# One encoder layer in split fp32: the order of the first down product, the place of X loads, and the step of a norm

## Chip, core and metric

The kernel runs on one core of a Trainium2 chip, as one launch. The metric is device time in microseconds: the median of the runs of one kernel. A profile of one execution lies beside it.

## The reference, cut to what matters

One layer is computed for 1024 prompt frames and 32 sample frames together (T = 1056 rows of width 1024): normalisation and projections, windowed attention and a gated recurrence, a mix, and then the part that this change touches:

```
[a | u] = RMSNorm(x) @ W_up            # 1024 -> 2 x 2816
a = causal depthwise conv3(a)
x = x + RMSNorm((gelu(a) * u) @ W_down)    # 2816 -> 1024, the "down product"
x = x + (p @ W_ple) * sigmoid(x @ W_ple_gate)
```

All of it is fp32. The kernel multiplies each pair of fp32 operands as a rounded high part and the rest: three matmuls (high by high, high by low, low by high) add up in one PSUM accumulator.

## The kernel before

The down product is worked out by Strassen's scheme: seven products (`i` = 0 to 6) of half-size blocks instead of eight. The operand of the product `i` that holds activations is called X(i); its sums were written to DRAM tiles `td` by the up stage. X(i) has three chunks (`KC`: 4, 4 and 3 blocks of 128 rows, index `j`), each in two halves `p` of 264 columns. A chunk's half is loaded by `x_in(i, q)` (q = 2j + p, one DMA on SyncE's queue, L1846) into a page of SBUF and then split by `x_parts`: ScalarE rounds it to the high part (L1835), VectorE subtracts (L1836). The pages of X(i) were those of X(i-2), so a load must wait until TensorE is done with these.

A product has four column blocks `c` of the output. A *step* is one (c, j): for both halves, 3 matmuls for each of the 4 or 3 blocks, so 24 or 18 matmuls (L2058 to L2060). Twelve steps make a product, 84 the whole stage (`QS`, counted as q). The results of a column block add up in one tile `st` of two PSUM banks, of which there are three; two more banks (`tr_bank`) serve transposes and small sums. In products 1 to 6 the steps go by c, and by j within c. In product 0 they go (0,0) (0,1) (1,0) (1,1) (2,0) (2,1), then the third chunk of blocks 0, 1 and 2, then the three steps of block 3: three `st` tiles allow three blocks to wait at a time. The third chunk of X(0) holds one k block that only the last up unit produces. It doesn't go through DRAM: VectorE computes it (L1696), and two DMAs on SyncE's queue copy it into place (L1698).

Each step needs weights. `w_in_(q)` loads one or two blocks of W_down (L1870; two in products 1 to 5), `w_parts(q)` adds the two on VectorE (L1877) and splits them as above into `wd`. In the program the load stands six steps ahead of its use and the split three. Raw weights of even q have two buffers (`wr`); those of odd q share eight (`wb`) with the split weights.

After block c, `d_out` adds or copies the result into the accumulators `acc` (ScalarE L1910, L1911, L1914; VectorE L1907). In product 4 `square` squares the finished blocks and adds them up on VectorE (`sqd`, L1937). Then `x2_first(t)`, t counted from product 5's step 0, does the norm of the first half of the columns: `x2_norm` (t = 3) sums the squares over partitions by twelve matmuls of one column (L1948) and takes the reciprocal root in a chain of small VectorE operations (L1949, L213 to L219); `x2_rows` (t = 7) turns the root into rows by six transposes (L303). Loads, sums and splits of the next stage's operand follow for t = 7 to 20.

The order is made by a planner: each instruction has the priority of its place in the program, and an instruction whose operands and buffers are free in the plan may be issued ahead of earlier ones that are not. On the chip each engine's queue, SyncE's for the DMAs included, then goes strictly in the planned order. `behind(e)` holds what is traced inside it behind the last instruction of engine e traced before; the call under it adds this tie only to instructions of that same engine:

```
ins = next(i for i in reversed(nc.cur_bb.bb.instructions) if i.engine == e.engine)
st.enter_context(tc.issue_after(ins))
```

After the seven products comes the gate stage (L2168 on), in which `y_start` loads a block of the per-layer input, `pl` (L2086).

Of the kernel before, what the change touches and what calls it, by code (L numbers as in the profile page):

```python
# [10 lines left out]
F32 = mybir.dt.float32  # L11
# [6 lines left out]
P = 128  # L18
# [12 lines left out]
H = 264  # L31
# [28 lines left out]
def layer_kernel(  # L60
# [17 lines left out]
    def nm(s):  # L78
        n_names[0] += 1
        return f"{s}_{n_names[0]}"  # L80
# [4 lines left out]
    dma, gdma = nc.sync.dma_start, nc.gpsimd.dma_start  # L85
    V, S, G, E = nc.vector, nc.scalar, nc.gpsimd, nc.tensor

    def behind(*engines):

        st = ExitStack()  # L90
        for e in engines:
            ins = next(i for i in reversed(nc.cur_bb.bb.instructions) if i.engine == e.engine)
            st.enter_context(tc.issue_after(ins))
        return st
# [29 lines left out]
    ple_d = dp.tile([P, 8, T], F32, name="ple_d")  # L124
# [115 lines left out]
    def tr_bank():  # L240
        return bank(pp, "tr", 2)
# [1436 lines left out]
    def down_parts(f, a, ab, out):  # L1678

        k, o4 = f // 2, halves(out)  # L1680
        neg = a[:, 0:T].rearrange("p (b a c) -> p b a c", b=2, a=2)[:, 0]
        b1, b2 = o4[:, :, 0, :], o4[:, :, 1, :]
        if f % 2 == 0:
            to_td(0, k, b1)
            to_td(3, k, b1)
            if f < NF - 2:
                S.mul(neg, b1, -1.0)
                to_td(2, k, neg)
            to_td(5, k, b1)
            to_td(6, k, b2)  # L1690
            add_td(5, k, b2)
            return
        if f == NF - 1:
            e1 = halves(Up[0][:, 0, :].bitcast(F32))[:, :, 0, :]
            d = a[:, 0:T].rearrange("p (b a c) -> p b a c", b=2, a=2)[:, 1]
            V.tensor_tensor(d, b1, e1, op=ALU.subtract)  # L1696
            for p in range(2):
                dma(X[0, p, 2][:, 1, 2, :].bitcast(F32), d[:, p])  # L1698
        S.mul(neg, b2, -1.0)
        to_td(1, k, b2)  # L1700
        to_td(4, k, b2)
        if f < NF - 1:
            add_td(2, k, b1)
        add_td(3, k, b2)
        add_td(4, k, b1)
        add_td(6, k, neg)
# [131 lines left out]
    X = {}  # L1838

    def x_in(i, q):  # L1840
        j, p = divmod(q, 2)
        n = KC[j][1]
        t = X[i, p, j] = page_at(SETS[i % 2][q], [P, 2, 4, H], "X")
        if (i, j) == (0, 2):
            n -= 1
        dma(t[:, 1, 0:n, :].bitcast(F32), td[TDI[i]][j][:, p, 0:n, :])  # L1846

    def x_parts(i, q):
        j, p = divmod(q, 2)
        to_parts(X[i, p, j], KC[j][1])  # L1850
# [4 lines left out]
          (A12, A22, ALU.subtract), (A21, A11, ALU.subtract), (A11,))  # L1855
    NQ = 84
    W = {}
    first_q = [(c, j) for c in range(3) for j in range(2)] + [(c, 2) for c in range(3)] + [(3, j) for j in range(3)]
    QS = [(i, c, j) for i in range(7)
          for c, j in (first_q if i == 0 else [(c, j) for c in range(4) for j in range(3)])]  # L1860

# [10 lines left out]
    def w_parts(q):  # L1872
# [3 lines left out]
        if len(WS[i]) > 1:  # L1876
            V.tensor_tensor(src, src, raw[:, 1, 0:n, :], op=WS[i][2])  # L1877
        to_parts(t, n, src)

    AHEAD_IN, AHEAD_PARTS = 6, 3  # L1880
    DOWN_AT = {0: [lambda: x_in(0, 0), lambda: x_in(0, 1)],
               1: [lambda: w_in_(1), lambda: x_in(0, 2), lambda: x_in(0, 3)],
               2: [lambda: w_in_(3), lambda: x_in(0, 4), lambda: x_in(0, 5), lambda: w_parts(0)],
# [18 lines left out]
    def d_out(i, c, b):  # L1902

        to = {k: a[:, c] for k, a in acc.items()}

        def add(key, op):
            V.tensor_tensor(to[key], to[key], b, op=op)  # L1907

        if i == 0:
            S.copy(to[0, 1], b)  # L1910
            S.copy(to[0, 0], b)  # L1911
        elif i == 1:
            add((0, 1), ALU.add)
            S.mul(to[1, 1], b, -1.0)  # L1914
        elif i == 2:
            add((0, 0), ALU.subtract)
            S.copy(to[1, 0], b)
        elif i == 3:
            add((0, 0), ALU.add)
            add((1, 1), ALU.add)  # L1920
        elif i == 4:
            add((0, 0), ALU.add)
        else:
            if i == 6:
                add((1, 0), ALU.add)
            add((1, 1), ALU.add)
# [36 lines left out]
    def cols_of(t, k, h):  # L1963
        return halves(t[:, k, :])[:, :, h, :]
# [20 lines left out]

    def x2_first(t):

        if t == 3:
            x2_norm(0)
        if t == 7:  # L1990
            with behind(E):
                x2_rows(0)
        if 7 <= t < 15:
            x2_load(0, t - 7)
        if 9 <= t < 17:
            x2_sum(0, t - 9)
        if 13 <= t < 21:
            x2_split(0, t - 13)
# [24 lines left out]
    for i in range(7):  # L2023
        for s, key in ACC_AT.get(i, ()):
            acc[key] = acc_page(s, "acc")
        bs = {}
        for s in range(12):
            q = 12 * i + s
            c, j = QS[q][1:]
            n = KC[j][1]  # L2030
            if j == 0:
                bs[c] = pf.tile([P, 2, 512], F32, tag="st", name=nm("st"), bufs=3)
            b = bs[c]
            if q == 1:
                finish_up()
                fctx.close()
                foctx.close()
                ep = ctx.enter_context(right("ep"))
            a = 4 if i == 0 else 0
            if i < 6 and a <= s < a + 6:  # L2040
                x_in(i + 1, s - a)
            if q + AHEAD_PARTS < NQ:
                w_parts(q + AHEAD_PARTS)
            if q + AHEAD_IN < NQ:
                w_in_(q + AHEAD_IN)
            if i == 0 and s in (4, 5):
                x_parts(0, s)
            a = 6 if i == 0 else 5
            if i < 6 and a <= s < a + 6:
                with behind(V) if i == 0 else ExitStack(), behind(S) if i == 0 else ExitStack():  # L2050
                    x_parts(i + 1, s - a)
            w = W.pop(q)
            for p in range(2):
                x = X[i, p, j]
                for k in range(n):
                    o = b[:, p, 0:H]
                    first, last = j == 0 and k == 0, j == 2 and k == n - 1
                    E.matmul(o, w[:, 0, k, :], x[:, 0, k, :], start=first, stop=False)  # L2058
                    E.matmul(o, w[:, 0, k, :], x[:, 1, k, :], start=False, stop=False)  # L2059
                    E.matmul(o, w[:, 1, k, :], x[:, 0, k, :], start=False, stop=last)  # L2060
            if i == 6:
                last_product(s)
            if i > 4:
                x2_first(12 * (i - 5) + s)
            if j < 2:
                continue
            d_out(i, c, bs.pop(c)[:, :, 0:H])
            if i == 2:
                square(0, 4 + c)
            elif i == 4:  # L2070
                square(0, c)
            elif i == 6:
                square(1, c)
                square(1, 4 + c)
# [8 lines left out]
    def y_start(h, c):  # L2083
        y = ep.tile([P, 2, H], F32, tag="t", name=nm("y"), bufs=4)
        pl = ep.tile([P, 2, H], F32, tag="pl", name=nm("pl"), bufs=2)
        dma(pl[:], cols_of(ple_d, c, h))  # L2086
        return y, pl

    def y_out(h, c, b, y, pl, z):
# [155 lines left out]
```

## Time and profile before

| | us |
|---|---|
| runs | 1988.96, 1985.16, 1987.40 |
| median | 1987.4 |
| the profiled execution's own time | 1984.17 |
| its span, first to last instruction | 1982.4 |
| TensorE's matmuls busy | 1947.6 |
| weight loads of TensorE busy | 1925.4 |
| VectorE busy | 1469.6 |
| ScalarE busy | 973.5 |
| down products (matmuls of L2058 to L2060) | 1631.28 to 1871.4 |

The profile's times are those of one execution, which is 3.2 us below the median of the runs. The down products take up 240 us near the end, and the gate stage the last 111. Two of the views need a word. A row of the timeline gives the start, the duration, engine, line, operation, what is written and read, and the form; in brackets stands the idle time of the engine before it and what ended it. A row of the stretches gives the busy time of each engine with the count of its instructions, then the granted clock of TensorE as a share of 2.4 GHz, the busy share of the 16 DMA engines, and what they moved.

### The profile page before, as it was taken

Reading aid. Unit: us, or ns where it says so; the run is one execution under the profiler, and the core shown is the slowest. Engines: PE = TensorE matmul, PEld = TensorE weight load, DVE = VectorE, ACT = ScalarE, POOL = GpSimd, SP = SyncE. Lnnn points to the kernel's source line nnn. Section 1 sums busy time; section 2 is a strip of 40 time slices with the busy share of each in tenths; the row PEclk is TensorE's granted clock in tenths of the full one; section 3 lists DMA queues with packets and bytes.
Section 4 is the critical chain, followed back from the end, with each engine's and each line's share of the span. In section 5 each row is a group of like instructions: output and inputs, shape, how many; then the busy total and the mean of one; then the engine's idle time right before and its main releaser. Section 6 shows DMA issues by size and latency. Waiting matters only on the chain. (4 is left out here: it accounts for less than half of the span.)

```text
span 1982.4 us, 38678 instructions
## 1 busy us (share of the span) xinstructions
PE 1947.6 (98%) x14715; PEld 1925.4 (97%) x14715; DVE 1469.6 (74%) x3194; ACT 973.5 (49%) x2207; POOL 289.6 (15%) x442
## 2 busy tenths in 40 slices
PE   7999999999999999999999999999999999999998
PEld 6999999999999999999999999999999999999998
DVE  6888888688888888553455778877788786678752
ACT  6655556556666666542124754333333335444432
POOL 2010100000000000002100013444554420000000
PEclk9999999999999999999999999999999999999999
DMA  9322311411111111377656693656465579889443
GB/s 270 105 84 84 104 62 54 154 47 58 38 54 42 50 55 57 122 238 228 188 169 212 212 316 99 140 125 143 112 138 134 129 189 275 239 259 278 137 116 83
DMA packets 334767, 277.58 MB, mean 140 GB/s; under 512 B 15925, under 2 KB 318136, under 8 KB 333941
## 3 DMA queue, kind: packets, MB, share of 16 engines
q1 hardware_dynamic: 312655, 234.67, 39.5%
q0 software_dynamic: 21856, 40.38, 9.2%
q8 instruction: 115, 1.88, 0.4%
q14 instruction: 71, 0.58, 0.1%
q10 hardware_dynamic: 70, 0.06, 0.0%
HBM read 186.21 MB, written 88.57 MB: 139 GB/s over the span
## 5 line engine op out<-in xcount | busy, mean ns | idle before, releaser
L1751 PE MATMUL st<-op,wt 128*128 128x264 f32 x1232 | 350.2, 284 | 3.1 <-DVE nr L219 1.0
L1753 PE MATMUL st<-op,wt 128*128 128x264 f32 x1232 | 349.6, 284 | 0.0
L1752 PE MATMUL st<-op,wt 128*128 128x264 f32 x1232 | 347.9, 282 | 0.0
L1751 PEld LDWEIGHTS st<-op,wt 128*128 128x128 f32 x1232 | 231.2, 188 | 6.0 <-DVE Sp L1769 1.7
L1752 PEld LDWEIGHTS st<-op,wt 128*128 128x128 f32 x1232 | 231.4, 188 | 0.0
L1753 PEld LDWEIGHTS st<-op,wt 128*128 128x128 f32 x1232 | 230.9, 187 | 0.0
L2058 PE MATMUL st<-X,wd 128*128 128x264 f32 x616 | 176.7, 287 | 1.8 <-ACT X L1835 1.8
L2060 PE MATMUL st<-X,wd 128*128 128x264 f32 x616 | 176.7, 287 | 1.6 <-DVE wd L1836 1.6
L2059 PE MATMUL st<-X,wd 128*128 128x264 f32 x616 | 176.2, 286 | 1.1 <-DVE X L1836 1.1
L202 PE MATMUL mm<-La,wh 128*128 128x384 f32 (+1 forms) x504 | 166.1, 330 | 0.3 <-ACT kt L342 0.3
L1519 ACT CAST wt<-wu 128x512 fp32r<-128x512 f32 x126 | 74.9, 619 | 181.5 <-POOL wu L1528 86.7
L203 PE MATMUL mm<-Lb,wh 128*128 128x384 f32 (+1 forms) x504 | 162.2, 322 | 0.0
L204 PE MATMUL mm<-La,wl 128*128 128x384 f32 (+1 forms) x504 | 162.1, 322 | 0.0
L202 PE MATMUL mm<-Ra,wh 128*128 128x264 f32 x512 | 145.4, 284 | 0.0
L203 PE MATMUL mm<-Rb,wh 128*128 128x264 f32 x512 | 145.0, 283 | 0.0
L204 PE MATMUL mm<-Ra,wl 128*128 128x264 f32 x512 | 145.0, 283 | 0.0
L1520 DVE TENSOR_TENSOR wt<-wu,wt 128x512 fp32r<-128x512 f32 x126 | 101.6, 808 | 47.5 <-ACT wt L1519 47.5
L2058 PEld LDWEIGHTS st<-X,wd 128*128 128x128 f32 x616 | 117.9, 191 | 2.3 <-ACT X L1835 2.3
L2060 PEld LDWEIGHTS st<-X,wd 128*128 128x128 f32 x616 | 117.6, 191 | 2.1 <-DVE wd L1836 2.1
L2059 PEld LDWEIGHTS st<-X,wd 128*128 128x128 f32 x616 | 117.8, 191 | 1.6 <-DVE X L1836 1.6
L186 DVE TENSOR_TENSOR wl<-wr,wh 128x1024 fp32r<-128x1024 f32 x62 | 75.9, 1224 | 42.0 <-ACT wh L183 40.4
L455 ACT ACTIVATE sc<-sc,st 128x257 f32<-128x257 f32 (+1 forms) x144 | 69.9, 487 | 71.9 <-DVE st L450 71.4
(493 smaller groups left out, 6040.3 us busy)
## 6 DMA issues: line engine op xcount, KB each, us to landing
wq<-in_w_down_dram SPq DMA_DIRECT2D x96, 256.0 KB
wu<-in_w_up_dram SPq DMA_DIRECT2D x42, 512.0 KB
td<-Up SPq DMA_DIRECT2D x66, 264.0 KB
wu<-in_w_in_dram SPq DMA_DIRECT2D x32, 512.0 KB
X<-td SPq DMA_DIRECT2D x28, 528.0 KB
wr<-in_w_in_dram SPq DMA_DIRECT2D x26, 512.0 KB
td<-Up POOLq DMA_DIRECT2D x43, 264.0 KB, 5.7
wq<-in_w_down_dram SPq DMA_DIRECT2D x48, 192.0 KB
```

What stands on the lines that cost most here:

```text
L186: V.tensor_tensor(lo[:], raw[:], hi[:].bitcast(F32), op=ALU.subtract)
L202: E.matmul(ps, wh, a, start=first and n == 0, stop=False)
L203: E.matmul(ps, wh, b, start=False, stop=False)
L204: E.matmul(ps, wl, a, start=False, stop=last and n == len(ks) - 1)
L1519: S.copy(t[:, 0], src)
L1520: V.tensor_tensor(t[:, 1], src, t[:, 0].bitcast(F32), op=ALU.subtract)
L1751: E.matmul(o, wh, xh, start=first and k == 0, stop=False, skip_group_check=True)
L1752: E.matmul(o, wh, xl, start=False, stop=False, skip_group_check=True)
L1753: E.matmul(o, wl, xh, start=False, stop=k == 3, skip_group_check=True)
L2058: E.matmul(o, w[:, 0, k, :], x[:, 0, k, :], start=first, stop=False)
L2059: E.matmul(o, w[:, 0, k, :], x[:, 1, k, :], start=False, stop=False)
L2060: E.matmul(o, w[:, 1, k, :], x[:, 0, k, :], start=False, stop=last)
```

## The change

1. *Order of the first product.* All four column blocks take chunks 0 and 1 first (eight steps), then the four take chunk 2. The fourth block adds up in two banks of `tr_bank` instead of an `st` tile, and is copied to the two accumulators by four ScalarE copies of one half each. The two DMAs of the last k block are issued from ScalarE's queue instead of SyncE's.
2. *Place of the X loads.* `x_in` of the next product's six half-chunks stands at steps 0, 2, 4, 6, 8, 9 (3, 5, 6, 8, 9, 10 in the first product) instead of 0 to 5 (4 to 9), inside `behind(E)`; the parts stand three steps later, in the next product's steps 0 and 1 for the last.
3. *The norm* moves from t = 3 to 5 and its rows from 7 to 8.
4. *The gate input's load* is put inside `behind(E)`.

```diff
             for p in range(2):
-                dma(X[0, p, 2][:, 1, 2, :].bitcast(F32), d[:, p])
+                S.dma_start(X[0, p, 2][:, 1, 2, :].bitcast(F32), d[:, p])
...
-    first_q = [(c, j) for c in range(3) for j in range(2)] + [(c, 2) for c in range(3)] + [(3, j) for j in range(3)]
+    first_q = [(c, j) for c in range(4) for j in range(2)] + [(c, 2) for c in range(4)]
...
+    X_IN = ((3, 5, 6, 8, 9, 10), (0, 2, 4, 6, 8, 9))
...
-        if t == 3:
+        if t == 5:
             x2_norm(0)
-        if t == 7:
+        if t == 8:
             with behind(E):
                 x2_rows(0)
...
-            if j == 0:
-                bs[c] = pf.tile([P, 2, 512], F32, tag="st", name=nm("st"), bufs=3)
+            if j == 0 and (i, c) == (0, 3):
+                bs[c] = [tr_bank()[:, 0:H] for _ in range(2)]
+            elif j == 0:
+                st = st_of[c] = pf.tile([P, 2, 512], F32, tag="st", name=nm("st"), bufs=3)
+                bs[c] = [st[:, p, 0:H] for p in range(2)]
...
-            a = 4 if i == 0 else 0
-            if i < 6 and a <= s < a + 6:
-                x_in(i + 1, s - a)
+            if i < 6 and s in X_IN[i > 0]:
+                with behind(E):
+                    x_in(i + 1, X_IN[i > 0].index(s))
...
-            a = 6 if i == 0 else 5
-            if i < 6 and a <= s < a + 6:
-                with behind(V) if i == 0 else ExitStack(), behind(S) if i == 0 else ExitStack():
-                    x_parts(i + 1, s - a)
+            for i_, t in ((i + 1, s), (i, 12 + s)):
+                if 0 < i_ < 7 and t - 3 in X_IN[i_ > 1]:
+                    n_ = X_IN[i_ > 1].index(t - 3)
+                    with behind(V) if i == 0 else ExitStack(), behind(S) if i == 0 else ExitStack():
+                        x_parts(i_, n_)
...
-            d_out(i, c, bs.pop(c)[:, :, 0:H])
+            if (i, c) == (0, 3):
+                for key in ((0, 1), (0, 0)):
+                    for p, o in enumerate(bs[c]):
+                        S.copy(acc[key][:, c, p], o)
+            else:
+                d_out(i, c, st_of[c][:, :, 0:H])
...
-        dma(pl[:], cols_of(ple_d, c, h))
+        with behind(E):
+            dma(pl[:], cols_of(ple_d, c, h))
```

## Rows read from the trace of the kernel before

**Rows 1.** The page's first part: busy time, share of the span, instructions.
```profile
PE 1947.6 (98%) x14715; PEld 1925.4 (97%) x14715; DVE 1469.6 (74%) x3194; ACT 973.5 (49%) x2207; POOL 289.6 (15%) x442
```

**Rows 2.** Stretches: first, second, fifth and sixth down product.
```profile
1631.28:1669.94 38.66, 35.76 (x267) 34.84 (x266) 26.15 (x37) 19.58 (x31) 3.29 (x3) 0.91 0.93 254
1669.94:1701.88 31.94, 31.94 (x266) 31.94 (x265) 21.73 (x32) 15.24 (x25) 0.00 (x0) 1.00 0.87 255
...
1765.78:1799.94 34.16, 32.52 (x266) 32.10 (x265) 25.92 (x39) 13.42 (x20) 0.00 (x0) 1.00 0.89 263
1799.94:1839.32 39.38, 36.39 (x284) 36.18 (x283) 33.46 (x61) 18.46 (x29) 0.00 (x0) 0.91 0.94 279
```

**Rows 3.** Who TensorE waited for, 1600 us to the end: total, times, longest.
```profile
PE tr L1948 <- DVE sqd L1937: 3.0, 1, 3.0
PE st L2058 <- ACT X L1835: 1.8, 2, 1.5
PE st L2060 <- DVE wd L1836: 1.6, 2, 0.8
PE st L2059 <- DVE X L1836: 1.1, 2, 0.6
```

**Rows 4.** Stretches, just after the first product's waits.
```profile
1654.00:1656.00 2.00, 2.00 (x9) 2.00 (x10) 1.71 (x2) 1.81 (x3) 0.00 (x0) 0.50 1.11 362
```

**Rows 5.** Timeline of TensorE, the first product's first wait.
```profile
1650.39 0.39 PE L2058 MATMUL st<-X,wd 128*128 128x264 f32 x1 [1.52 <-ACT X L1835]
```

**Rows 6.** Timeline of SyncE, end of the last up unit.
```profile
1644.80 1.72 SPq L1698 DMA_DIRECT2D X<-a  x2
...
1649.54 1.33 SPq L2086 DMA_DIRECT2D pl<-ple_d  x2
```

**Rows 7.** Timeline of VectorE, third X chunk of the first product.
```profile
1650.37 0.98 DVE L1836 TENSOR_TENSOR X<-X 128x792 fp32r<-128x792 f32 x1 [3.38 <-ACT X L1835]
1652.95 0.98 DVE L1836 TENSOR_TENSOR X<-X 128x792 fp32r<-128x792 f32 x1 [1.60 <-ACT X L1835]
```

**Rows 8.** Who SyncE waited for, 1665 to 1870 us.
```profile
SPq L1870 <- DVE wd L1836: 70.4, 31, 5.1
```

**Rows 9.** Stretches of 4 us in the third and fourth product.
```profile
1724.00:1728.00 4.00, 4.00 (x35) 4.00 (x34) 3.38 (x6) 2.18 (x4) 0.00 (x0) 1.00 0.50 138
...
1748.00:1752.00 4.00, 4.00 (x36) 4.00 (x35) 3.72 (x5) 2.97 (x4) 0.00 (x0) 1.00 1.11 338
```

**Rows 10.** Timeline of VectorE, parts of the weights of steps 21 and 41.
```profile
1686.45 0.69 DVE L1836 TENSOR_TENSOR wd<-wq,wd 128x512 fp32r<-128x512 f32 x1
...
1746.67 0.55 DVE L1836 TENSOR_TENSOR wd<-wq,wd 128x384 fp32r<-128x384 f32 x1
```

**Rows 11.** Timeline of TensorE, first matmuls of steps 21 and 41.
```profile
1693.90 0.28 PE L2058 MATMUL st<-X,wd 128*128 128x264 f32 x1
...
1747.63 0.28 PE L2058 MATMUL st<-X,wd 128*128 128x264 f32 x1
```

**Rows 12.** Timeline of TensorE, sums of squares, first and second norm.
```profile
1813.98 1.92 PE L1948 MATMUL tr<-ones,sqd 128*88 128x1 f32 x12 [2.99 <-DVE sqd L1937]
...
1883.19 1.03 PE L1948 MATMUL tr<-ones,sqd 128*88 128x1 f32 x12
```

**Rows 13.** Timeline of VectorE, sixth product.
```profile
1816.13 1.25 DVE L1836 TENSOR_TENSOR X<-X 128x1056 fp32r<-128x1056 f32 x1
...
1822.88 0.15 DVE L1949 TENSOR_SCALAR nv<-tr 88x6 f32<-88x6 f32 x1
...
1828.23 0.17 DVE L219 SCALAR_TENSOR_TENSOR nr<-rst,nr 128x6 f32<-128x6 f32 x1
```

**Rows 14.** One tile (st) from 1600 to 1720 us: copies of a finished block.
```profile
L1910 ACT COPY acc<-st x4: 589/598/612, 1658.9 to 1671.8; 128x528 f32<-128x528 f32 x4
```

**Rows 15.** Timeline of SyncE, fifth product.
```profile
1772.33 0.45 SPq L1846 DMA_DIRECT2D X<-td  x1
1772.87 0.94 SPq L1870 DMA_DIRECT2D wq<-in_w_down_dram  x2
```

More of the change, by code (lines that the diff above doesn't have):

```diff
@@ L2025, in layer_kernel @@
             acc[key] = acc_page(s, "acc")
-        bs = {}
+        bs, st_of = {}, {}
         for s in range(12):
@@ L2055, in layer_kernel @@
                 for k in range(n):
-                    o = b[:, p, 0:H]
+                    o = b[p]
                     first, last = j == 0 and k == 0, j == 2 and k == n - 1
```

## The prediction

> **What bounds the kernel now.** I read the page's busy shares first: TensorE is busy for 98% of the span [rows 1], so only its idle and slow stretches can be won. Second, the table of stretches, one per down product [rows 2]: 264 matmuls take 31.94 us in the second product (the third and fourth are alike), so a matmul has a slot of 31.94/264 = 0.121 us, a step of 24 takes 2.91 us and one of 18 takes 2.18. The first product lasts 38.66 us, the fifth 34.16, the sixth 39.38: 6.7, 2.2 and 7.4 us over. Third, who TensorE waits for from 1600 us on [rows 3]: 7.5 us in seven waits, plus 0.5 at the very end, which the change doesn't touch. The excess of 16.3 us is twice the waiting: after the first product's waits the granted clock is 0.50, the 1.2 GHz level [rows 4], and matmuls go at half pace until it returns. So a stall's price is read from a stage's excess. Last, what those waits wait for.
>
> *First product.* TensorE is free at 1650.39 - 1.52 = 1648.87 and waits for the third X chunk [rows 5]. Its last k block comes from the last up unit by two DMAs issued from 1644.80 [rows 6]; VectorE finishes the halves of the chunk at 1651.35 and 1653.93 [rows 7]. Three steps with that chunk stand next in order.
>
> *Fifth product.* Weights come just too late. SyncE waits 70.4 us in all, 31 times, for VectorE to free a weight buffer [rows 8]. While X is loaded the DMA share is 1.11 at 338 GB/s, and between such times 0.50 at 138 [rows 9]: weight loads meet X loads in a bunch. VectorE ends the parts of step 21 (first multiplied at 1693.90) at 1687.14, a lead of 6.8 us; those of step 41 (1747.63) at 1747.22, a lead of 0.4 [rows 10, 11].
>
> *Sixth product.* The norm's twelve small matmuls wait 2.99 us for the sum of squares and then run in 1.92 us, against 1.03 at full clock [rows 12].
>
> **The change, part by part.**
>
> *A: first product reordered.* It removes nothing; the fourth block's steps of chunks one and two (2.91 us each) move ahead of the third chunk. That chunk is then needed at 1648.87 + 5.82 = 1654.7, its second half 9 matmuls (1.09 us) later, at 1655.8. It is there at 1651.35 and 1653.93: 3.3 and 1.9 us to spare. So the whole excess goes: **-6.7 us**. The weights of the moved steps keep their place in the sequence of loads, only their contents change. The two banks belong to a pool used before the last 21 up units and again from the sixth product on, so nobody else wants them. The block is copied out by four half-size copies instead of two of 0.60 us [rows 14]: between 0 and 1.2 us more of ScalarE, behind which stand casts that the second product needs later; nothing, and 1.2 if that cover is gone.
>
> The two DMAs of the last k block go to ScalarE's queue. On SyncE issuing them took 1.72 us [rows 6]; ScalarE had idle time there, while behind it stand the negation, a weight cast and an X cast. SyncE's next three weight loads can go up to 1.72 us sooner. I take 0 for both, with 1.7 as bound on either side; the 1.9 to spare just covers the worse one. The Trainium skill, "DMA: Bandwidth & Descriptors", section "Issuing engines are not separate DMA queues", says that such a move saves only the sequencer's issuing time and that the transfers still share the same engines. By that rule the chunk lands no sooner and A rests on the reordering alone; if a queue of its own helped, the spare time would grow and the sum stay. No run here shows which.
>
> Does A last? The weights must be 6.7 us sooner too. In the second product the lead is 6.8 us or more, but it falls to 0.4 by step 41. With weights arriving at unchanged times A would be eaten there: A is worth between 0 and -6.7, according to the next part.
>
> *B: X loads spread.* Six loads in steps 0, 2, 4, 6, 8, 9 instead of 0 to 5, the parts three steps later. In the trace X and weight loads alternate, one X to each pair, in program order [rows 15]; a later place lets weight loads go first. No load is added. But the wrapper put around them names TensorE's last instruction and ties only what the same engine issues; these blocks hold a SyncE DMA alone. So nothing is tied to TensorE, and only the place in the program works. The planner lets a DMA whose buffer is free go early: the first two gate inputs, 220 us before use, went at 1649.54 [rows 6]. So the spreading is partial, the gate inputs stay where they are (0 us), and the second product's X loads, whose buffers come free with the last up unit, go ahead of their place as before. Partial is enough if a pair of weights meets two thirds of an X load: the DMA then sits between its two shares. I take the weights to keep up: the fifth product's **-2.2 us**, and A lasts. Bounds: nothing of either, and all of both.
>
> *C: norm at step 5 instead of 3, its rows after step 8 instead of 7.* Step 4 and 5 (2.91 + 2.18) then cover the 2.99 wait. Of the 7.4 excess 1.4 is work that stays (1.03 for the norm [rows 12], the rest the rows' six transposes), so **-6.0** gross. What is late next is the reciprocal root. After the norm's matmuls end (1815.90) VectorE starts it only at 1822.88 and ends at 1828.40 [rows 13]: 12.5 us, because parts of weights and of X stand ahead of it and between its steps in that queue. TensorE used to have four steps for that and gets three: 2.91 + 2.91 + 2.17 = 8.0 us. If nothing shortens the chain the wait is 4.5. Four X parts stand within the chain, two of 1.25 us [rows 13] and two of 0.98 [rows 7], 4.5 in sum; with the loads spread about half fall behind it, leaving 2.3. I take 3.4. A wait of 2.99 had cost 6.0 in all, so 3.0 go on top for the slow clock: 6.4. C comes to +0.4, between -6.0 (no wait) and +1.5.
>
> Sum: -6.7 - 2.2 + 0.4 = **-8.5 us**. The profiled execution took 1984.17 (span 1982.4 and 1.8 around it): 1975.7 by it. The median shown is 1987.4, 3.2 above, so I forecast 1987.4 - 8.5 = **1978.9**.
>
> **Rivals.**
>
> 1. *Everything lands.* The root is ready in time since weights lead again by 8 us or more. Then -6.7 - 2.2 - 6.0 = -14.9: 1972.5. For it: leads of 6.8 us existed at step 21. Against: the root's chain is 12.5 us long now, with VectorE almost without gaps in it.
>
> 2. *The weights set the pace.* X loads stay where their buffers come free, since the ties are empty, and A is paid back at steps 41 to 60 in many small waits; VectorE's queue, unmoved, ends the root at 1828.4 or later, so step 69 starts when it did. -6.7 + 6.7 for A, 0 for B, C between 0 and -2: 1986.4. For it: the lead of 0.4 and the half-empty DMA at 1724, which says that buffers, not bandwidth, hold the weights back there. Against: the alternation in program order.
>
> 3. *The last X chunk comes late: slower.* With its load at step 9 and its parts at step 12, which is step 0 of the next product, the second half is needed at that product's step 2. VectorE takes it behind the parts of weights up to three steps ahead. While the weights lead by less than some 3 us (one step), that order makes X late by about a step less the lead, 2.66 - 1.1 = 1.5 us, and the slow clock doubles it: 3 us in each of the third to sixth products, 12 in all, against A's 6.7 alone: +5.3, so 1992.7. It decides from the point at which the lead is under one step. For it: leads near zero from step 41 to 63. Against: the planner takes X parts as soon as they land.
>
> **How the numbers follow.** Forecast 0.48, with a range of its own from 1975 to 1983; rival 1 0.13, rival 2 0.25, rival 3 0.14. 0.2% is 4 us, about what a measurement of this kernel can tell. Faster by more: 0.45 of the forecast, all of rival 1 and 0.03 of rival 2, 0.61. Within: 0.03 + 0.18 + 0.01 = 0.22. Slower: 0.04 of rival 2 and 0.13 of rival 3, 0.17. The range holds rivals 1 and 2 and the near half of rival 3: 1972 to 1989.5; about 0.05 lies below and 0.12 above.
>
> **What would show it.** A: no wait of the first product for X, and its stage at 32 us. B: the DMA share between 0.7 and 1.0 throughout the second to fifth products, fewer X loads side by side with each pair of weights, leads of two steps or more at steps 41 to 60. C: no wait for the sum of squares; the transposes of the norm's rows waiting for the root by 2 to 5 us, then a granted clock of 0.50. The prediction is wrong if the X loads keep their alternation and the leads still fall to zero (rival 2), if TensorE waits for X at step 2 of a product (rival 3), or if the first product still stalls at step 8.

## The result, and the profile after

The changed kernel takes 1995.79 us, median of 5 runs (1994.41 to 1999.03), against 1986.68 for the kernel before beside it (1983.72 to 1988.96): ratio 1.0050, 95% interval 1.0035 to 1.0064. It is slower by 9 us; forecast were 1978.9, and 1972 to 1989.5.

The profiled execution took 1999.03 (span 1997.0). The seven down products in it last from 1639.13 to 1886.02, 246.9 us against 240.2 before (1631.28 to 1871.44). By these two executions 6.7 us arise in this stage; the medians lie 9.1 apart. The rest cannot be placed: the gate stage behind takes 111.0 in both, and the stage began 7.9 us later in that execution than in the one of before, but its beginning varies between executions (last section). I therefore compare stages, each of them from one execution.

Stretches of the kernel after, for the first, second, fourth, fifth and sixth product, then three short ones. Columns: stretch and length, busy time of TensorE, its weight loads, VectorE, ScalarE and GpSimd with counts, granted clock, DMA share, GB/s.

```profile
1639.13:1675.76 36.63, 32.11 (x266) 31.90 (x265) 23.08 (x33) 16.51 (x26) 3.29 (x3) 0.96 0.94 260
1675.76:1709.72 33.96, 33.96 (x265) 33.96 (x266) 21.48 (x32) 17.26 (x30) 0.00 (x0) 0.94 0.78 227
1741.84:1777.66 35.82, 34.02 (x266) 33.60 (x265) 24.56 (x37) 12.96 (x19) 0.00 (x0) 0.95 0.84 253
1777.66:1811.67 34.01, 32.80 (x267) 32.17 (x265) 24.82 (x37) 13.29 (x20) 0.00 (x0) 1.00 0.89 261
1811.67:1853.91 42.24, 35.20 (x285) 34.99 (x283) 33.04 (x60) 17.59 (x28) 0.00 (x0) 0.92 0.89 260
...
1676.00:1678.00 2.00, 2.00 (x10) 2.00 (x11) 1.52 (x2) 0.68 (x1) 0.00 (x0) 0.50 0.99 340
...
1736.00:1740.00 4.00, 4.00 (x35) 4.00 (x34) 3.77 (x7) 1.87 (x4) 0.00 (x0) 1.00 0.37 106
...
1756.00:1760.00 4.00, 2.40 (x12) 2.19 (x13) 3.40 (x5) 2.08 (x5) 0.00 (x0) 0.81 1.08 372
```

A product without a stall takes 31.94 [rows 2]. Over that, before and after: first 6.7 and 4.7, second 0 and 2.0, fourth 0 and 3.9, fifth 2.2 and 2.1, sixth 7.4 and 10.3. The excess moved and grew.

Who TensorE waited for from 1600 us on (total, times, longest):

```profile
PE tr L303 <- DVE nr L219: 7.0, 1, 7.0
PE st L2063 <- ACT acc L1912: 4.5, 1, 4.5
PE st L2063 <- ACT wd L1835: 2.1, 2, 1.5
PE st L2065 <- DVE wd L1836: 0.9, 2, 0.6
```

The busy shares are those of [rows 1] within a point and tell nothing of it. Against [rows 3], the waits that the change aimed at, for X and for the sum of squares, are gone. Two longer ones stand in their place: for the copies of a finished block (L1912), and for the norm's reciprocal root (L219).

*The copies.* TensorE multiplied block 0 for the last time at 1664.7 (step 8 now, step 6 before). ScalarE's timeline, and the matmul that waits:

```profile
1669.02 0.62 ACT L1835 CAST wd<-wq 128x512 fp32r<-128x512 f32 x1 [4.92 <-DVE wd L1836]
1669.55 2.29 ACT L1835 CAST X<-X 128x1056 fp32r<-128x1056 f32 x2
1671.74 0.61 ACT L1835 CAST wd<-wq 128x512 fp32r<-128x512 f32 x1
1674.20 0.51 ACT L1835 CAST wd<-wq 128x384 fp32r<-128x384 f32 x1 [1.84 <-DVE wd L1836]
1674.62 0.59 ACT L1911 COPY acc<-st 128x528 f32<-128x528 f32 x1
1675.11 0.60 ACT L1912 COPY acc<-st 128x528 f32<-128x528 f32 x1
...
1675.76 0.59 PE L2063 MATMUL st<-X,wd 128*128 128x264 f32 x1 [4.52 <-ACT acc L1912]
```

The copies start 9.9 us after their data is there. Ahead of them stand three weight casts, the last of them for step 14, and two X casts; twice ScalarE stands idle (4.92 and 1.84 us) before a weight cast that waits for VectorE's work on the weights. The second product needs the same PSUM buffer. Before, block 0's first copy went at 1658.9 [rows 14], 11 us ahead of that need. Where the clock is 0.50 after the wait, the 1.2 GHz level, the second product loses its 2.0.

*The root.* The norm's matmuls end at 1828.7 without a wait. VectorE:

```profile
1838.22 0.98 DVE L1836 TENSOR_TENSOR X<-X 128x792 fp32r<-128x792 f32 x1 [0.63 <-ACT X L1835]
1839.12 0.69 DVE L1836 TENSOR_TENSOR wd<-wq,wd 128x512 fp32r<-128x512 f32 x1
1839.88 0.98 DVE L1836 TENSOR_TENSOR X<-X 128x792 fp32r<-128x792 f32 x1
1840.78 0.70 DVE L1908 TENSOR_TENSOR acc<-acc,st 128x528 f32<-128x528 f32 x1
1841.39 0.15 DVE L1950 TENSOR_SCALAR nv<-tr 88x6 f32<-88x6 f32 x1
...
1843.59 0.17 DVE L219 SCALAR_TENSOR_TENSOR nr<-rst,nr 128x6 f32<-128x6 f32 x1
```

It starts the root 12.7 us after the matmuls (7.0 before [rows 13]), behind the seventh product's last two X parts, and behind three sums of weights that waited 3.1 us in all for their loads. The chain of waits leads on from the second of these X parts to its load (start, length, what):

```profile
1833.11 5.86 DMA X<-td
1838.99 0.86 ACT X L1835
1839.88 0.98 DVE X L1836
```

*The fourth product* has a stall that before did not show. ScalarE again, and TensorE's matmul at step 41:

```profile
1751.94 1.08 ACT L1835 CAST X<-X 128x1056 fp32r<-128x1056 f32 x1 [2.56 <-DMA X<-td]
1755.22 1.07 ACT L1835 CAST X<-X 128x1056 fp32r<-128x1056 f32 x1 [2.20 <-DMA X<-td]
...
1756.69 0.51 ACT L1835 CAST wd<-wq 128x384 fp32r<-128x384 f32 x1
...
1757.25 0.39 PE L2063 MATMUL st<-X,wd 128*128 128x264 f32 x1 [1.46 <-ACT wd L1835]
```

The weight cast that TensorE waits for stands behind two X casts that wait for their loads to land, and this X is multiplied from 1777.66 on, 20 us later. The same two casts stood ahead of step 41's weights in the kernel before, where nothing stalled:

```profile
1741.37 1.08 ACT L1835 CAST X<-X 128x1056 fp32r<-128x1056 f32 x1 [2.79 <-DMA X<-td]
1744.38 1.08 ACT L1835 CAST X<-X 128x1056 fp32r<-128x1056 f32 x1 [1.93 <-DMA X<-td]
```

So the order in this queue is not new. What is new is that the weights come later: counted from the stage's beginning, TensorE reaches the fourth product at 102.6 us before and 102.7 after, and ScalarE starts step 41's weight cast at 114.8 before and 117.6 after. It is one pattern three times: work that TensorE needs now stands in an engine's queue behind work that it needs later, whose data is not there.

### The profile page after: what moved, and what is told of

Same layout as the page of the kernel before. It is cut to its first block, busy times and chain, and to the rows that moved or that the text cites. A ratio compares the mean times of both kernels' runs of the same rounds, so it can differ in the third digit from the quotient of the medians.

```text
span 1997.0 us, 38675 instructions
## 1 busy us (share of the span) xinstructions
PE 1953.2 (98%) x14715; PEld 1930.1 (97%) x14715; DVE 1468.9 (74%) x3194; ACT 971.2 (49%) x2209; POOL 289.0 (14%) x442
## 4 chain that ended last, share of the span: by engine, by line
PE 56%; issue 14%; DMA 8%; DVE 7%; POOL 5%; ACT 4%; SPq 1%; POOLq 0%; DVEq 0%; ACTq 0%
PE mm L202 4%; PE mm L203 3%; PE mm L204 3%; PE st L2065 3%; DMA td<-Up 3%; PE st L2063 3%; PE st L2064 3%; PE st L1751 3%; PE st L1753 2%; PE st L1752 2%; PE G L843 2%; PE Y L840 2%; PE G L842 2%; PE Y L842 2%; PE G L840 2%
## 5 line engine op out<-in xcount | busy, mean ns | idle before, releaser
L2063 PE MATMUL st<-X,wd 128*128 128x264 f32 x594 | 170.6, 287 | 6.6 <-ACT acc L1912 4.5
L2065 PE MATMUL st<-X,wd 128*128 128x264 f32 x594 | 170.7, 287 | 0.9 <-DVE wd L1836 0.9
L2064 PE MATMUL st<-X,wd 128*128 128x264 f32 x594 | 169.8, 286 | 0.0
L2063 PEld LDWEIGHTS st<-X,wd 128*128 128x128 f32 x594 | 113.8, 192 | 7.2 <-ACT acc L1912 4.7
L2065 PEld LDWEIGHTS st<-X,wd 128*128 128x128 f32 x594 | 113.5, 191 | 1.7 <-DVE wd L1836 1.6
L2064 PEld LDWEIGHTS st<-X,wd 128*128 128x128 f32 x594 | 113.8, 192 | 0.0
```

## The experiments

*Theory 1.* The order in each engine's queue is laid out for parts that run four and five steps ahead. On the chip the weights' lead (from the end of VectorE's split to the first matmul) is -1.0 to 4.3 us from step 29 to step 63 of the changed kernel, less than two steps, so what follows from a matmul (copies, root) stands behind parts that come late; the change only moves the stall. *Rivals* (numbered anew, they are not the prediction's): the spread X loads alone cost (2); the supply of weights sets the pace and any order gives the same end (3); the kept order tried below wins by itself (4); the whole's loss is made up in another way than by B lengthening the root's wait (5). Each kernel is compared with the kernel before on the same chip; "stage" is the seven products of the profiled execution (240.2 before, 246.9 after).

```
kernel                          median    ratio to before, 95%        stage
A alone (e1_order)              1989.02   1.0019 (1.0004 to 1.0035)   242.4
B alone (e1_xplaces)            1988.05   1.0007 (0.9995 to 1.0019)   242.1
C alone (e1_norm)               1988.32   1.0007 (0.9996 to 1.0019)   243.7
after, without C (e1_nonorm)    1990.50   1.0019 (1.0007 to 1.0031)   244.1
after, without B (e4_no_b)      1990.64   1.0021 (1.0009 to 1.0033)   245.9
after, old X6 (e4_x6_old)       1992.85   1.0038 (1.0025 to 1.0051)   248.6
after, DMAs SyncE (e3_syncdma)  1995.99   1.0037 (1.0024 to 1.0051)   245.2
after, e2_tied_copies           1988.23   1.0014 (1.0003 to 1.0026)   241.6
after, e2_tied_root             1995.61   1.0049 (1.0035 to 1.0062)   247.7
after, e3_root_x                1986.86   1.0000 (0.9987 to 1.0012)   237.7
after, e2_rows11                1988.71   1.0019 (1.0008 to 1.0031)   240.0
all in order (e2_tied_all)      1977.84   0.9955 (0.9942 to 0.9968)   234.0
before, in order (e3_before_tied)1983.81  0.9979 (0.9966 to 0.9992)   238.9
in order, e3_tied_early         1979.55   0.9953 (0.9939 to 0.9968)   234.1
in order, e4_tied_no_c          1979.13   0.9964 (0.9953 to 0.9975)   230.9
in order, e4_tied_no_b          1980.37   0.9970 (0.9957 to 0.9983)   233.3
```

**The parts alone, and the change less a part.** A alone is the new `first_q` and the two spare banks; B alone `X_IN` with its parts; C alone is

```diff
-        if t == 3:
+        if t == 5:
             x2_norm(0)
-        if t == 7:
+        if t == 8:
```

> Edit: the kernel before with the reordered first product and its two spare banks alone (X loads, norm and the two DMAs as before). Theory 1 (a stall moves to what hangs on TensorE's results): the X wait of the first product is gone, TensorE waits 3 to 5 us for the copies of block 0 at the start of the second product instead, because they stand in ScalarE's queue behind weight casts; the end moves by less than 3 us: 1984 to 1990. Rival 2 (the spread X loads are what costs): the reordering by itself keeps most of its 6.7 us: 1979 to 1982. Rival 3 (the weights alone set the pace): no wait for block 0, the gain is paid back in waits for weights from step 40 on: 1986 to 1988.

> Edit: the kernel before with the new places of the X loads and X parts alone. Theory 1: the first product is as before; leads of the weights fall to 0 to 2 us already at steps 30 to 40, with new waits there of 1 to 3 us, and the norm's root ends later by 1 to 4 us without TensorE noticing at first: 1986 to 1992. Rival 2 (these places are what costs): 1993 to 1997. Rival 3 (weights alone set the pace): 1985 to 1988. As the prediction had it: 1984.5.

> Edit: the kernel before with the norm's matmuls at step 5 and its rows after step 8 of the sixth product alone. Theory 1: the wait for the sum of squares (2.99 us) is gone, the transposes of the norm's rows wait for the root by 3 to 5 us, less than the 7.0 of the whole change since the last X loads are in their old places; the sixth product takes 38.5 to 41 us against 39.38: 1986 to 1989. Rival 2: wait under 2 us, 1981 to 1984. Rival 3 (this edit alone brings the loss): wait of 7 us or more, 1989 to 1992.

> Edit: the changed kernel with the norm's matmuls and rows back at steps 3 and 7. Theory 1: the wait for the sum of squares comes back (about 3 us), the root still comes late because the last X parts stand ahead of it, so the rows' transposes at step 7 wait too: 1991 to 1995. Rival 2 (the spread X loads cost the root and this is all there is to it): 1989 to 1991. Rival 3 (the norm's new place is no matter): 1995 to 1997.

No part gains, and A loses. Each is in theory 1's range, but two not as it said. With B alone the leads at steps 30 to 40 were 2.6 to 6.4 us, not 0 to 2, and the cost lies in the fifth product (36.4 against 34.2). With C alone the sixth product took 43.6, not 38.5 to 41.

A alone has the copies' wait already, with the X loads in their old places (ScalarE, then TensorE):

```profile
1668.10 0.51 ACT L1835 CAST wd<-wq 128x384 fp32r<-128x384 f32 x1 [0.93 <-DVE wd L1836]
1668.52 0.59 ACT L1911 COPY acc<-st 128x528 f32<-128x528 f32 x1
...
1669.66 0.39 PE L2062 MATMUL st<-X,wd 128*128 128x264 f32 x1 [3.67 <-ACT acc L1912]
```

That fells rival 2, under which A would have kept its 6.7. C alone turns the wait for the sum of squares into one for the root:

```profile
PE tr L303 <- DVE nr L219: 4.4, 1, 4.4
```

Its sixth product is longer than in the whole change (42.24), with waits for weights of 2.2 us beside this one:

```profile
1805.65:1849.27 43.62, 36.96 (x285) 36.12 (x284) 33.32 (x60) 17.76 (x28) 0.00 (x0) 0.92 0.86 253
```

A alone also has the fourth product's stall, at the same step:

```profile
1751.76 0.39 PE L2062 MATMUL st<-X,wd 128*128 128x264 f32 x1 [1.13 <-ACT wd L1835]
```

Its fourth product takes 33.95, with B alone 32.14. So the spread X loads are not what makes this stall.

Without C the whole is at 1990.50, inside what rival 2 expected: the wait for the sum of squares is back (2.8), but the rows, which theory 1 let wait too, do not. Do the losses add up? By the medians of their own comparisons A costs 2.1, B 1.1, C 1.4, 4.6 in sum, where the whole costs 9.1. By the ratios it is 0.33% against 0.50%, with intervals that don't part the two, and by the stages 2.2, 1.9 and 3.5, 7.6 in sum, against 6.7. So whether the parts cost more together than apart is not settled.

**B's share in the root's wait.** `e4_no_b` puts the X loads back into their old places, `e4_x6_old` only those of the seventh product:

```diff
-            if i < 6 and s in X_IN[i > 0]:
+            if i == 5 and s < 6:
+                x_in(6, s)
+            elif i < 5 and s in X_IN[i > 0]:
```

> Edit: the changed kernel with X loads and X parts back in their old places (steps 0 to 5 and 5 to 10). Theory 1 (the spread X loads delay the root): the transposes wait 3.5 to 5 us as with the norm's new place alone (4.4), not 7.0; the copies still make the second product wait 3.5 to 4.5: 1989 to 1992. Rival 5 (the parts' losses add up otherwise): 1994 to 1997.

> Edit: the changed kernel with the X loads and parts of the seventh product alone back in their old places. Theory 1 (it is these loads that delay the root): the transposes wait 3.5 to 5 us, 1990 to 1993. Rival 5: 1994 to 1997.

Their waits for the root, `e4_no_b` first, then `e4_x6_old`:

```profile
PE tr L303 <- DVE nr L219: 4.3, 1, 4.3
```

```profile
PE tr L303 <- DVE nr L219: 4.7, 1, 4.7
```

So the last X loads alone lengthen the root's wait from 4.7 to 7.0. Four kernels with these loads spread wait 5.3 to 7.5 us (the change, `e3_syncdma`, `e2_tied_copies`, `e2_tied_root`), three with them in the old places 4.3 to 4.7. Rival 5 falls for the wait: both runs lie in theory 1's range. (The copies' wait in `e4_no_b` is 2.9, shorter than the 3.5 to 4.5 expected.) The worth in time is not settled: `e4_x6_old` is at 1.0038 where the change is at 1.0050, and these intervals overlap; weight waits elsewhere were longer in its profile, and its stage longer than the changed kernel's. In `e4_no_b` the sixth product takes 43.3, no less than with B.

**The two DMAs of the last k block** back on SyncE:

```diff
-                S.dma_start(X[0, p, 2][:, 1, 2, :].bitcast(F32), d[:, p])
+                dma(X[0, p, 2][:, 1, 2, :].bitcast(F32), d[:, p])
```

> Edit: the changed kernel with the two DMAs of the last k block back in SyncE's queue. Theory 1: ScalarE's queue starts its casts for steps 10 and 11 up to 1.7 us sooner, SyncE's loads later by as much; the wait for block 0's copies stays at 3.5 to 5 us: 1994 to 1997. Rival (the two DMAs in ScalarE's queue are what makes the copies late): that wait under 2 us and 1989 to 1992.

The copies' wait stays (4.7), and the time cannot be told from the change's (1.0037 and 1.0050, with overlapping intervals). Issuing took 1.48 us on ScalarE (kernel after) and 1.41 on SyncE:

```profile
1653.31 1.48 ACTq L1698 DMA_DIRECT2D X<-a  x2
```

```profile
1653.08 1.41 SPq L1698 DMA_DIRECT2D X<-a  x2
```

**The order kept in one place.** Parts of weights, and in some kernels of X, are tied to their place in the program on VectorE and ScalarE, under a condition:

```diff
+            tied = ...
             if q + AHEAD_PARTS < NQ:
-                w_parts(q + AHEAD_PARTS)
+                with behind(V) if tied else ExitStack(), behind(S) if tied else ExitStack():
+                    w_parts(q + AHEAD_PARTS)
...
-                    with behind(V) if i == 0 else ExitStack(), behind(S) if i == 0 else ExitStack():
+                    with behind(V) if i == 0 or tied else ExitStack(), behind(S) if i == 0 or tied else ExitStack():
                         x_parts(i_, n_)
```

`e2_tied_copies`: `i == 0 and s > 8`, weights on ScalarE alone, with the third product's X parts; `e2_tied_root`: `i == 5 and s > 5`; `e3_root_x`: the same, and all X parts of the seventh product. `e2_rows11` instead moves the rows of the norm, and the sums and splits behind them:

```diff
-        if t == 8:
+        if t == 11:
             with behind(E):
                 x2_rows(0)
...
-        if 9 <= t < 17:
-            x2_sum(0, t - 9)
-        if 13 <= t < 21:
-            x2_split(0, t - 13)
+        if 12 <= t < 20:
+            x2_sum(0, t - 12)
+        if 14 <= t < 22:
+            x2_split(0, t - 14)
```

> Edit: the changed kernel, but from step 9 of the first product on weight casts, and X parts for the third product, are kept in program order on their engines, so that ScalarE copies block 0 before it casts weights four and five steps ahead. Theory 1 (a result of TensorE stands in a queue behind weights that come late): the wait of 4.5 us for the copies at the start of the second product shrinks to under 1 us and most of the 6.7 us comes back: 1988 to 1991. Rival 3 (the weights alone set the pace): the wait is gone but comes back as waits for weights in the third to fifth products: 1994 to 1997.

> Edit: the changed kernel, but in the sixth product from step 6 on the parts of weights and of X are kept in program order, so that VectorE does the norm's root before parts for steps four and five ahead. Theory 1: the root ends some 3 to 6 us sooner, the transposes of the norm's rows wait 1 to 4 us instead of 7.0, the sixth product takes 36 to 40 us instead of 42.2: 1990 to 1993. Rival 3: the wait goes but weights come late instead, sixth product 41 to 43 us: 1995 to 1997.

> Edit: as the kernel with the kept order in the sixth product from step 6, and X parts for the seventh product kept in program order too, the last one among them, which stood alone ahead of the root there (VectorE idle 9.47 us for it). Theory 1 (the last X load holds the root): the root no longer waits for that load, the transposes wait under 2 us instead of 7.5, the sixth product takes 33 to 36 us: 1986 to 1990. Rival 3 (weights set the pace): no change of the time, 1994 to 1997.

> Edit: the changed kernel with the transposes of the norm's rows after step 11 instead of 8, the sums from step 12 and the splits from step 14. Theory 1: no wait for the root, the sixth product takes 33 to 35 us: 1986 to 1989. Rival: the sums and splits, now later, stand in VectorE's queue at the end and the gate waits for them by as much: 1993 to 1997.

With the copies in order they start at 1659.22, right behind the block's last matmul, and 6 to 7 us come back. They do not come back where theory 1 had them. The second product has a new wait of 4.5 us, for an X part now behind weights, and the first two products lose 7.8 us in place of 6.7. What is won lies in the fourth and fifth: the third to fifth products take 31.95 each, and step 41's weights lead by 3.3 us. So the fourth product's stall goes with the copies' order, though the spread X loads are still there. It also speaks against rival 3, under which waits for weights would have come in these products. Later rows bring 4 to 6 us: no wait for the root is left, but the rival to this run is right in part. TensorE waits 0.9 us for ScalarE (`yr`) in the gate stage, which takes 113.6 us in place of 111.0.

`e2_tied_root` missed: 7.5 us of wait as before. Its VectorE, and ScalarE at that time, show why:

```profile
1823.27 0.70 DVE L1908 TENSOR_TENSOR acc<-acc,st 128x528 f32<-128x528 f32 x1
1833.43 0.98 DVE L1836 TENSOR_TENSOR X<-X 128x792 fp32r<-128x792 f32 x1 [9.47 <-ACT X L1835]
...
1834.94 0.15 DVE L1950 TENSOR_SCALAR nv<-tr 88x6 f32<-88x6 f32 x1
```

```profile
1832.55 0.85 ACT L1835 CAST X<-X 128x792 fp32r<-128x792 f32 x1 [9.79 <-DMA X<-td]
```

The one X part whose place in the program lies in the seventh product was not tied and went ahead. VectorE stands idle for 9.47 us before it, while the root's input has been there since 1823.2, when the norm's matmuls end. The Trainium skill, "PSUM — Partial Sum Buffer", section "Engine vs sequencer instructions", says that the queues of ScalarE and VectorE are strictly first in, first out; the 9.47 us of idling with ready work behind agree. `e3_root_x` ties that part too; the root's first and last instruction there:

```profile
1823.83 0.15 DVE L1950 TENSOR_SCALAR nv<-tr 88x6 f32<-88x6 f32 x1
...
1827.46 0.17 DVE L219 SCALAR_TENSOR_TENSOR nr<-rst,nr 128x6 f32<-128x6 f32 x1
```

TensorE has no wait for it at all, the sixth product takes 33.5 us instead of 42.2, and the kernel is level with before. The places of the seventh product's X parts were worth 9 us against `e2_tied_root`.

**The order kept everywhere** (`tied = q > 8`), in the changed kernel, in the kernel before, and with one thing altered: the norm at steps 3 and 7, the X loads in their old places, or earlier:

```diff
-    X_IN = ((3, 5, 6, 8, 9, 10), (0, 2, 4, 6, 8, 9))
+    X_IN = ((3, 4, 5, 6, 7, 8), (0, 1, 3, 4, 6, 7))
```

> Edit: the changed kernel with all parts of weights and of X from step 9 on kept in program order on VectorE and ScalarE, three steps ahead of TensorE. Theory 1: both waits shrink (copies under 1 us, root under 4 us) and the sum is 8 to 14 us better: 1982 to 1988. Rival 3 (weights set the pace): three steps of order leave less room for late weights, new waits for weights in every product: 1996 to 2010.

> Edit: the kernel before with all parts of weights and of X from step 9 on kept in program order on VectorE and ScalarE, and nothing of the change. Theory 1 (the change frees waits, but only an order kept on the two engines lets them stay free): the first product keeps its 6.7 us for the third X chunk and the norm its wait for the sum of squares; only the waits in the fifth product go: 1981 to 1986, so the change is worth 4 to 8 us under the kept order, where it cost 9 without. Rival 4 (the kept order is a gain by itself that has nothing to do with the change): 1974 to 1979, as the changed kernel with it.

> Edit: the changed kernel with the kept order everywhere, and X loads at steps 0, 1, 3, 4, 6 and 7 instead of 0, 2, 4, 6, 8 and 9 (in the first product 3 to 8), parts three steps later as before. Theory 1: with the kept order what is left are waits for X parts at steps 1 to 3 of the second and sixth products (4.1 us in sum, some 8 of excess); parts two steps sooner remove most of them: 1970 to 1975. Rival (spread loads are what keeps the weights up): weights fall behind while X is loaded, 1977 to 1984.

> Edit: the changed kernel with the kept order everywhere and the norm back at steps 3 and 7. Theory 1: the wait for the sum of squares comes back with at most 3 us and 3 of slow clock, none for the root: 1978 to 1984, so the norm's new place is worth 0 to 6 us under the kept order. Rival: no difference to the kept order with it, 1977 to 1979, since X parts are what is late there.

> Edit: the changed kernel with the kept order everywhere and the X loads and parts in their old places. Theory 1: the waits for late X parts in the second and sixth products go (parts two steps sooner), others for weights come in the fourth, fifth and seventh as in the kernel before with the kept order: 1977 to 1982. Rival (the spread loads are what makes the kept order work): 1983 to 1988.

`e2_tied_all` is 7 to 9 us faster than before (by medians and by ratio) and 16 to 19 faster than the change, better than the 1982 to 1988 that theory 1 expected. Its first, second and sixth product, ScalarE's first copy of block 0, and TensorE's waits for X:

```profile
1631.93:1663.88 31.95, 31.95 (x267) 31.95 (x266) 18.92 (x27) 15.83 (x27) 3.29 (x3) 1.00 1.00 280
1663.88:1700.24 36.36, 34.03 (x266) 33.61 (x265) 25.44 (x36) 17.34 (x28) 0.00 (x0) 0.95 0.85 243
...
1796.42:1833.78 37.36, 35.52 (x284) 35.12 (x283) 30.98 (x57) 17.38 (x28) 0.00 (x0) 0.95 0.92 262
```

```profile
1657.56 0.61 ACT L1911 COPY acc<-st 128x528 f32<-128x528 f32 x1 [1.40 <-PE st L2067]
```

```profile
PE st L2065 <- ACT X L1835: 3.0, 2, 1.8
PE st L2066 <- DVE X L1836: 1.1, 2, 0.6
```

ScalarE now waits for TensorE before the copies, not for weights, and the first product has no excess: the 31.94 that was forecast. That fells rival 3: the same weights and the same loads come in time. Rival 4 is right by about half: the same order gives 0.9979 in the kernel before and 0.9955 in the changed one (their intervals touch). So the change is worth about 5 us under the kept order, where it costs 9 without. In the kernel before the kept order also took away the wait for the sum of squares, which theory 1 had expected to stay.

Of that gain A's share can be seen in the stage. The first product takes 31.94 us in all four kernels with A under the kept order and 36.9 in the kernel before with it. `e4_tied_no_b`, which has A and no B, loses nothing in the second either:

```profile
1632.90:1664.85 31.95, 31.95 (x267) 31.95 (x266) 19.15 (x26) 15.94 (x25) 3.29 (x3) 1.00 1.00 284
1664.85:1696.79 31.94, 31.94 (x266) 31.94 (x265) 23.77 (x34) 17.32 (x30) 0.00 (x0) 1.00 0.92 256
```

So an order kept on the two engines is what A lacked. What B and C are worth there is not settled. Without C 0.9964, without B 0.9970, and X loads earlier 0.9953 cannot be told from 0.9955. For C, the wait for the sum of squares that theory 1 expected back did not come back. The earlier X loads were expected at 1970 to 1975 and missed: the X waits above went, and waits for weights, 3.6 us in sum, came, most of it in the third and fifth products. A without B and C was not tried under this order.

## Why the prediction was wrong

*The first failed step is the price of A's copies* ("nothing, and 1.2 if that cover is gone") and with it "the whole excess goes". I priced the fourth block's copies by their length, and asked when X is there. Block 0's copies, which A makes later, had no term: I did not ask when their buffer is needed again, nor what stands ahead of them in ScalarE's queue. With block 0 complete at step 8 the second product needs its buffer three short steps later, 6.5 us, and the copies came after 9.9. Measured: 4.7 in the first product and 2.0 in the second, all of A's 6.7. With the order kept and no B, both are nothing (`e4_tied_no_b`). The X wait itself went, as forecast. "A is paid back", in the prediction's rival 2, was right on the sum, wrong on the place: in the change it is one wait for a buffer, not many small ones for weights.

*The second is "I take the weights to keep up"*, by which B was to bring 2.2 and A to last. The fifth product's 2.2 stayed (2.1), and the fourth gained 3.9: at step 41, where the lead was 0.4 [rows 10, 11], TensorE now waits. The sign that the prediction named was there to see. The DMA share did not stay between 0.7 and 1.0 but swung from 0.37 to 1.08 within 24 us, beside 0.50 and 1.11 before [rows 9]; the six X loads of the fourth product went out from 5.9 to 20.4 us after its beginning, before from 3.1 to 15.8. So the loads were hardly spread. Yet the fourth product's loss is not B's. It is there with A and old X places (2.0), not with B alone (0.2), and gone with B in place and the copies in order (0.0). A's copies or what stands around them made the weights late up to there; by which path was not followed.

*The third is C's size.* The 6.0 us for the sum of squares went, and the root became the next wait, as forecast. The bound "if nothing shortens the chain the wait is 4.5" is what C alone shows, 4.4; from the norm's matmuls to the root's end it is 12.5 us there as before. What failed is "with the loads spread about half fall behind it, leaving 2.3": the parts kept their place ahead of the root and only came later, 7.0 instead of 3.4. The sixth product's excess is 10.3, against 7.8 forecast. C alone has 11.7 with a shorter wait for the root, since TensorE also waits 2.2 us for weights there; C's sum had no term for that.

Sum: forecast -8.5, stage +6.7. The difference of 15.2 is 6.7 (first and second product), 3.9 and 2.1 (fourth and fifth) and 2.5 (sixth).

*Right:* ScalarE's issuing of the two DMAs costs or gains nothing that can be told. The gate inputs' loads stayed where they were in the stage (1656.74 after, 1649.54 before [rows 6], with a stage that began 7.9 later). That the ties around the X loads are empty was argued from the program and not tried by itself. The prediction's rival 3, X late at step 2 of a product, did not happen in the changed kernel. It did under the kept order, at step 2 of the second and sixth products (1.8 and 1.2 us).

## What to carry to other kernels

When a wait is removed by reordering, ask for every buffer that is freed later when it is next written, and read the queue of the engine that frees it: what matters is not how long its copy takes but whose late data stands ahead of it. Here an order planned with a longer lead than the chip gave put far-off work ahead of urgent work on ScalarE and VectorE; before moving loads, tie the parts to their place and see how many waits go. A wait that is gone is not yet time won: look at where the next products lose or gain, and at the stage behind, before a gain is put down to it.

## What the runs showed of the hardware

A stage's beginning moves between executions though TensorE's instructions up to it are the same in their order: the first down product began between 1631.3 and 1639.1 us in the profiled executions of all these kernels. In the one of the changed kernel the first 50 us had a mean granted clock of 0.85, in that of before 1.00:

```profile
0.00:50.00 50.00, 36.05 (x163) 28.63 (x164) 27.71 (x80) 28.86 (x54) 11.81 (x29) 0.85 0.84 259
```

For an effect of half a per cent this is as large as the effect, so stages tell more than spans; but a stage, too, is from one execution.

The slow clock after a stall has a price of its own, which did not grow with the wait in these four stalls. Excess over the wait (in the sixth product also less the 1.5 us that it takes longer with no wait at all, 33.46 in `e3_root_x`): 1.8 us behind 3.7 (A alone), 2.2 behind 4.5 and 1.7 behind 7.0 (the change), 2.9 behind 2.99 (before). Of the longest wait, a part of the slow clock lies within the wait, where it costs nothing:

```profile
1841.00:1843.80 2.80, 0.00 (x0) 0.00 (x0) 2.42 (x14) 0.28 (x1) 0.00 (x0) 0.50 0.99 290
```

The prediction's doubling of a wait is near for the wait of 2.99 us and too much for the one of 7.
